# Row sums of 16384 x 1024 floats: one block of 128 rows a partition with one store, in place of blocks of 112 and 16 rows with a store each

## The chip, the cores and the metric

The kernel runs on one core of a Trainium2 chip. Its input lies in HBM, the chip's main memory, and is worked on in SBUF, the memory beside the core's engines, which has 128 partitions; DMA engines move the data between them in packets. SyncE and ScalarE issue these transfers; VectorE and ScalarE do the sums. The metric is device time in microseconds (us); lower is better. A time is some 1.8 us longer than the span of its profile (162.43 against 160.6 us for the profiled run of before), so differences carry over from one to the other.

## The reference

```python
def setup_inputs():
    batch, seq, dim = 32, 512, 1024
    return {"x": np.random.randn(batch, seq, dim).astype(np.float32)}

def reference(x):
    return np.sum(x, axis=-1).astype(np.float32)
```

67.1 MB are read and 64 KB are written. There is one addition for every four bytes read; the profile below shows that the reading sets the time.

## The kernel before

The 16384 rows are dealt to 128 partitions. A *block* with n rows a partition gives partition p the rows p*n to p*n + n - 1 of that block, so neighbouring partitions start n * 4 KiB apart in HBM. This distance is called the *pitch* below. A tile is 16 rows a partition, 64 KiB each, 8.39 MB in all.

```python
BLOCKS = (112, 16)
G = 16                                   # rows a partition in one tile
...
xpool = ctx.enter_context(tc.tile_pool(name="x", bufs=3))
...
def block(r0, n):
    x_b = x_flat[r0 : r0 + P * n].rearrange("(p c) d -> p (c d)", p=P)
    out_b = out_flat[r0 : r0 + P * n].rearrange("(p c) -> p c", p=P)
    return x_b, out_b, rpool.tile([P, n], F32, name=f"res{r0}")

for b, n in enumerate(BLOCKS):
    x_b, out_b, res = block(done * P, n)
    final = b == len(BLOCKS) - 1
    whole = n - G if final else n
    while c < whole:                     # seven whole tiles in all
        ...  # load of 16 rows from SyncE, reduce on VectorE;
        ...  # in the seventh tile ScalarE sums 7 of the 16 rows
    if not final:
        nc.scalar.dma_start(out=out_b, in_=res)      # 112 columns, 448 B a partition
    done += n

# the last tile: loads of 9, 4 and 2 rows and of two parts of a row;
# VectorE and ScalarE share its rows
...
nc.sync.dma_start(out=out_b, in_=res)                # 16 columns, 64 B a partition
```

The seven whole tiles are at a pitch of 448 KiB, the last one, the block of 16 rows, at 64 KiB.

## Time and profile before

| | before |
|---|---|
| time, median of the first 3 runs | 162.22 us (162.12 to 162.32) |
| span of the profile | 160.6 us |
| first whole reduce starts | 22.00 us |
| from one whole reduce to the next | 19.35 us |
| last store issued | 158.36 us |

The page of the kernel before: the span, the two DMA queues (packets, MB, share of the span of 16 engines) and the chain of work that ended last, by engine and by line.

```profile
span 160.6 us, 119 instructions
...
q1 hardware_dynamic: 2016, 67.12, 97.2%
q10 hardware_dynamic: 144, 0.06, 0.1%
...
DMA 75%; DVE 23%; SPq 0%; issue 0%; DVEq 0%
DMA xt<-in_x_dram 75%; DVE res L43 21%; DVE pairs L59 1%; SPq L95 0%; DVE seen L112 0%; DVE part L59 0%; DVE res L59 0%; DVEq L120 0%
...
```

The load queue is busy for 97.2% of the span, and waits for a load make up 75% of the span in the chain. The 23% on VectorE look like a second limit, but the timeline shows that they are not. Here are some of its VectorE lines for before: start, duration, engine, line, operation, operands, and in brackets how long VectorE had been idle and what ended that.

```profile
...
start us, us, engine line op out<-in xcount [idle before <-releaser]
22.00 17.22 DVE L43 TENSOR_REDUCE res<-xt 128x16 f32<-128x16384 f32 x1 [22.00 <-DMA xt<-in_x_dram]
41.27 17.22 DVE L43 TENSOR_REDUCE res<-xt 128x16 f32<-128x16384 f32 x1 [2.06 <-DMA xt<-in_x_dram]
60.63 17.22 DVE L43 TENSOR_REDUCE res<-xt 128x16 f32<-128x16384 f32 x1 [2.13 <-DMA xt<-in_x_dram]
...
138.03 9.75 DVE L43 TENSOR_REDUCE res<-xt 128x9 f32<-128x9216 f32 x1 [2.13 <-DMA xt<-in_x_dram]
...
156.58 0.69 DVE L59 CUSTOM_DVE_ANT_0 pairs<-xt 128x512 f32<-128x512 f32 x1 [0.25 <-DMA xt<-in_x_dram]
...
```

Each whole reduce takes 17.22 us, and then VectorE waits about 2.1 us for the next tile. A tile arrives every 19.35 us, so 8.39 MB / 19.35 us = 434 GB/s. The Trainium skill, "DMA: Bandwidth & Descriptors", section Specifications, gives 435 GB/s as the fabric ceiling, the limit at SBUF's ports; the trace agrees.

The line of the last store in the same timeline, and the list of DMA issues (out<-in, issuing queue, KB, us from issue to landing):

```profile
...
158.36 0.35 SPq L114 DMA_DIRECT2D out_dram<-res  x1
```

```profile
...
issues: line engine op xcount, KB each, median us to landing
xt<-in_x_dram SPq DMA_DIRECT2D x1, 7680.0 KB, 21.5
...
out_dram<-res ACTq DMA_DIRECT2D x1, 56.0 KB, 7.5
out_dram<-res SPq DMA_DIRECT2D x1, 8.0 KB, 1.4
```

### The profile page before, as it was taken

The numbers are of one execution on the slowest core, as the hardware profiler recorded it, in microseconds if no ns is written. First come the engines' busy times: TensorE is split into PE (matmuls) and PEld (weight loads), VectorE is DVE, ScalarE is ACT, GpSimd is POOL, SyncE is SP. The second block draws the span as 40 slices with busy tenths as digits, with TensorE's granted clock in tenths as the row PEclk, the third lists the DMA queues.
The fourth block names the chain that finished last, engine by engine and source line by source line (L and its number), as shares of the span: only waits on it lengthen the run. The fifth ranks groups of instructions, "written<-read, shape, count | busy, mean of one in ns | idle before, by whom it ended". The sixth has DMA issues, their size and how long they took to land.

```text
span 160.6 us, 119 instructions
## 1 busy us (share of the span) xinstructions
DVE 121.5 (76%) x16; ACT 17.2 (11%) x31; POOL 0.2 (0%) x4
## 2 busy tenths in 40 slices
DVE  0000059997799959999499994999949998697884
ACT  0000000000000000000000000000000000695892
POOL 0000000000000000000000000000000000000000
DMA  9988996996996996996996996996996996998991
GB/s 375 490 367 367 490 522 277 506 522 277 506 522 261 522 522 261 522 522 261 522 506 277 522 506 277 522 506 277 522 506 277 522 490 294 441 431 364 436 390 44
DMA packets 2160, 67.18 MB, mean 418 GB/s; under 512 B 496, under 2 KB 624, under 8 KB 880
## 3 DMA queue, kind: packets, MB, share of 16 engines
q1 hardware_dynamic: 2016, 67.12, 97.2%
q10 hardware_dynamic: 144, 0.06, 0.1%
HBM read 67.11 MB, written 0.07 MB: 418 GB/s over the span
## 4 chain that ended last, share of the span: by engine, by line
DMA 75%; DVE 23%; SPq 0%; issue 0%; DVEq 0%
DMA xt<-in_x_dram 75%; DVE res L43 21%; DVE pairs L59 1%; SPq L95 0%; DVE seen L112 0%; DVE part L59 0%; DVE res L59 0%; DVEq L120 0%
## 5 line engine op out<-in xcount | busy, mean ns | idle before, releaser
L43 DVE TENSOR_REDUCE res<-xt 128x16 f32<-128x16384 f32 (+3 forms) x9 | 119.8, 13309 | 36.5 <-DMA xt<-in_x_dram 36.5
L51 ACT ACT_TABLE_LOAD x1 | 1.3, 1283 | 138.1 <-DMA xt<-in_x_dram 138.1
L51 ACT ACTIVATE xt<-xt 128x1024 f32<-128x1024 f32 x15 | 15.6, 1044 | 2.4 <-DMA xt<-in_x_dram 2.3
L51 ACT ACTIVATION_READ_ACCUMULATOR xt<-xt 128x1 f32 x15 | 2.8, 187 | 0.0
L59 DVE CUSTOM_DVE_ANT_0 pairs<-xt 128x512 f32<-128x512 f32 (+1 forms) x2 | 1.1, 567 | 0.2 <-DMA xt<-in_x_dram 0.2
L59 DVE CUSTOM_DVE_ANT_0 pairs<-xt,part 128x240 f32<-128x240 f32 x1 | 0.5, 468 | 0.0
L112 DVE COPY seen<-part 128x1 f32<-128x1 f32 x1 | 0.2, 153 | 0.0
L59 DVE DVE_READ_ACCUMULATOR2_ANT res<- 128x1 f32 x2 | 0.2, 83 | 0.0
L157 POOL MEMSET const-uint8-127<- 128x1 uint8 x1 | 0.1, 102 | 0.0
L157 POOL MEMSET const-bfloat16-1.0<- 128x1 bf16 x1 | 0.1, 101 | 0.0
L157 POOL MEMSET const-float32-0.0<- 128x1 f32 x1 | 0.1, 99 | 0.2 <-issue 0.2
L157 POOL MEMSET const-float32-1.0<- 128x1 f32 x1 | 0.1, 99 | 0.0
L59 DVE DVE_READ_ACCUMULATOR2_ANT part<- 128x1 f32 x1 | 0.1, 83 | 0.0
## 6 DMA issues: line engine op xcount, KB each, us to landing
xt<-in_x_dram SPq DMA_DIRECT2D x1, 7680.0 KB, 21.5
xt<-in_x_dram SPq DMA_DIRECT2D x1, 4608.0 KB, 32.5
xt<-in_x_dram SPq DMA_DIRECT2D x1, 2048.0 KB, 37.1
xt<-in_x_dram SPq DMA_DIRECT2D x1, 1024.0 KB, 39.1
xt<-in_x_dram SPq DMA_DIRECT2D x1, 512.0 KB, 3.8
xt<-in_x_dram SPq DMA_DIRECT2D x1, 272.0 KB, 39.3
xt<-in_x_dram SPq DMA_DIRECT2D x1, 240.0 KB, 39.4
xt<-in_x_dram SPq DMA_DIRECT2D x6, 40.8
```

The lines of the kernel that those rows point to most:

```text
L43: nc.vector.tensor_reduce(out=res[:, c : c + n], in_=xt[:, j * D : (j + n) * D].rearrange("p (j d) -> p j d", d=D), axis=X, op=ADD,)
L51: nc.scalar.activation(out=v, in_=v, func=COPY, accum_out=acc)
L59: nc.vector.tensor_tensor_reduce(out=pairs[:, 0 : h - a], in0=xt[:, a:h], in1=xt[:, h:b], scale=1.0, scalar=first, op0=ADD, op1=ADD, accum ...
L112: nc.vector.tensor_copy(out=seen, in_=part)
L157: nc = _bacc.Bacc("TRN2", target_bir_lowering=False, num_devices=1)
```

## The change

The intent is one DMA less: the results are kept until the end and stored at once, 512 B a partition. The early store no longer runs among the last loads.

```diff
-BLOCKS = (112, 16)
+BLOCKS = (128,)
```

This one line also moves the rows: every tile is now at a pitch of 512 KiB. Which partition sums which row changes, the result doesn't. The tiles, their sizes and the work of each engine stay as they were.

## The prediction

> **What bounds the kernel now.** The loads do. The page gives the load queue 97.2% of the 16 DMA engines' span. The chain of waits is 75% "DMA xt<-in_x_dram". Its 23% on VectorE is not a limit: the timeline shows the 17.22 us tile reduces starting every 19.35 us (41.27, 60.63, 79.97, 99.32 us), each after a 2.13 us wait for a load. A tile is 8.39 MB, so 19.35 us is 434 GB/s. The Trainium skill, "DMA: Bandwidth & Descriptors", section Specifications, gives a fabric ceiling of 435 GB/s; the trace agrees. In the packet records every 64 KiB packet takes 2.42 us (10th to 90th percentile 2.418 to 2.43), in the 112-row block, whose partitions start 448 KiB apart, and in the 16-row block, 64 KiB apart, alike.
>
> **What the change does.**
> 1. It removes the store of 112 columns that ScalarE issued at 147.87 us: 128 packets of 448 B, 8 on each engine, 25 ns each in the packet records. They ran between the last loads and hold each engine for 8 x 25 ns = 0.20 us. The last loads should land 0.20 us earlier; that is on the critical path. The 0.37 us of issue on ScalarE is not: it waits afterwards for a load until 149.07 us.
> 2. It makes the last store 64 KB instead of 8 KB, 512 B a partition instead of 64 B. The 64 B packets take 11 ns. A line through 64 B (11 ns) and 448 B (25 ns) gives 27 ns for 512 B, so 8 packets take 0.22 us instead of 0.09 us: +0.13 us, an estimate, fully exposed after the last reduce. The rest of its 1.4 us from issue to landing stays.
> 3. It moves the rows in HBM. The partitions of every tile now start 512 KiB apart, a power of two. The packets (64 KiB) and all work of VectorE and ScalarE stay the same.
>
> Items 1 and 2 sum to about -0.07 us, below the run-to-run spread (162.12 to 162.32 us).
>
> Item 3 is the risk. The same page, section Latency and other measured facts, reports 207 GB/s for copies between HBM tensors with a row pitch of 512 KiB, against 214 GB/s with a padded pitch, and a far larger loss from 2 MiB on. If that 3% applied to this one-way read, the loads' 155 us would become 160 us, and the kernel would take 167 us. I do not expect it: HBM is only read here, in 64 KiB runs, and the engines seem to set the 2.42 us. No run of this case shows it yet.
>
> **Prediction.** 162.1 us, within 161.7 to 163.4 us 8 times in 10. Faster by over 2%: 1%. Within 2%: 82%. Slower by over 2%: 17%.
>
> **What the profile would show.**
> - Item 1 right: the second DMA queue is gone; the wait of the first pair reduction (156.58 us) ends about 0.2 us earlier, and so does the issue of the last store (158.36 us).
> - Item 2 right: that store goes from 1.4 us to about 1.5 us between issue and landing; the span after its issue (2.3 us) grows by about 0.13 us.
> - Item 3 harmless: 64 KiB packets stay at 2.42 us, tile reduces 19.35 us apart. Harmful: the spacing grows in all tiles alike, towards 20 us, with longer packets and longer waits of VectorE for the loads.
>
> **What would make it wrong.** A loss from the 512 KiB pitch in the reads (slower by 1 to 4%); a last store whose 512 B writes finish much later or sooner than that line says. A gain over 2% would need loads above 434 GB/s, and nothing in the change can give that.

## The result, and the profile after

| | before | after |
|---|---|---|
| time, median of 6 runs each | 162.27 us (162.12 to 162.49) | 162.76 us (162.58 to 162.94) |
| ratio of the times | | 1.003, 95% interval 1.0018 to 1.0043 |

A ratio here is the mean time of one kernel's fast runs over that of the other's of the same rounds, so it is not quite the ratio of the medians. The difference of 0.49 us is small, but clear of the noise.

The page of the kernel after, the same lines:

```profile
span 161.0 us, 118 instructions
...
q1 hardware_dynamic: 2016, 67.18, 97.2%
...
DMA 75%; DVE 22%; SPq 0%; issue 0%; DVEq 0%
DMA xt<-in_x_dram 75%; DVE res L43 21%; DVE pairs L59 1%; SPq L95 0%; DVE seen L112 0%; DVE part L59 0%; DVEq L120 0%; DVE res L59 0%
...
```

The second queue is gone and the shares are the same: the page cannot show where 0.4 us went. The VectorE lines of the timeline can (after):

```profile
...
start us, us, engine line op out<-in xcount [idle before <-releaser]
22.39 17.22 DVE L43 TENSOR_REDUCE res<-xt 128x16 f32<-128x16384 f32 x1 [22.39 <-DMA xt<-in_x_dram]
41.66 17.22 DVE L43 TENSOR_REDUCE res<-xt 128x16 f32<-128x16384 f32 x1 [2.06 <-DMA xt<-in_x_dram]
61.02 17.22 DVE L43 TENSOR_REDUCE res<-xt 128x16 f32<-128x16384 f32 x1 [2.14 <-DMA xt<-in_x_dram]
...
138.43 9.75 DVE L43 TENSOR_REDUCE res<-xt 128x9 f32<-128x9216 f32 x1 [2.13 <-DMA xt<-in_x_dram]
...
156.72 0.69 DVE L59 CUSTOM_DVE_ANT_0 pairs<-xt 128x512 f32<-128x512 f32 x1 [0.20 <-DMA xt<-in_x_dram]
...
```

```profile
...
158.54 0.35 SPq L114 DMA_DIRECT2D out_dram<-res  x1
```

```profile
...
issues: line engine op xcount, KB each, median us to landing
xt<-in_x_dram SPq DMA_DIRECT2D x1, 7680.0 KB, 21.9
...
out_dram<-res SPq DMA_DIRECT2D x1, 64.0 KB, 1.5
```

The first whole reduce starts 0.39 us later. From there everything keeps pace: 41.66 to 61.02 us is again a spacing of about 19.35 us. At the end some of the delay comes back. Four stretches make up the span: S up to the start of the first whole reduce, M from there to the reduce of 9 rows, E from there to the issue of the last store, T from there to the end of the span. Their sums differ from the span by rounding only.

| us | S | M | E | T | span |
|---|---|---|---|---|---|
| before | 22.00 | 116.03 | 20.33 | 2.29 | 160.65 |
| after | 22.39 | 116.04 | 20.11 | 2.49 | 161.03 |

So the start costs 0.39 us, E gains 0.22 us, T costs 0.20 us, and the 116 us in the middle, six tiles at full rate, do not change at all.

The packet records of the DMA engines show the start finer. Of the first tile, one row comes in packets of 4 KiB, and then the other 15 rows as one DMA, in packets of 60 KiB, eight rounds of one packet on each of the 16 engines. The packets sorted by start, in groups of 16, mean duration in us, from both traces:

```
                    round 1  round 2  round 3  round 4   packets over 2.3 us
before                 2.27     2.27     2.27     2.27     0 of 128
after                  2.63     2.40     2.39     2.27    30 of 128
```

After the change the first three rounds are slow, and from the fourth on the packets take 2.27 us as before. The very first packets, of 4 KiB, differ too: before, the first six started 0, 5, 14, 17, 18 and 46 ns after the earliest, and after the change 0, 55, 103, 172, 224 and 282 ns. (The records do not name the engine of a packet; a round here is only the order of the starts.)

### The profile page after: what moved, and what is told of

Same layout as the page of the kernel before. It is cut to its first block, busy times and chain, and to the rows that moved or that the text cites. A ratio compares the mean times of both kernels' runs of the same rounds, so it can differ in the third digit from the quotient of the medians.

```text
span 161.0 us, 118 instructions
## 1 busy us (share of the span) xinstructions
DVE 121.5 (75%) x16; ACT 17.1 (11%) x31; POOL 0.2 (0%) x4
## 4 chain that ended last, share of the span: by engine, by line
DMA 75%; DVE 22%; SPq 0%; issue 0%; DVEq 0%
DMA xt<-in_x_dram 75%; DVE res L43 21%; DVE pairs L59 1%; SPq L95 0%; DVE seen L112 0%; DVE part L59 0%; DVEq L120 0%; DVE res L59 0%
```

## The experiments

**Theory A:** the pitch of 512 KiB makes the loads collide as long as all engines start together, and only then; the stores nearly cancel. Rivals: **N**, the late first tile was the luck of one profile; **S**, the larger last store costs the 0.5 us; **F**, only the first touch of HBM is slow; **B**, something else in the block of 128 rows costs it, not its pitch.

Twelve kernels ran. They ran in four batches, each on another chip: late_store, blocks_64_64, one_buffer_before and one_buffer_after in one, the two at 508 KiB in one, the two at 448 KiB in one, the rest in one. The kernel before was timed again in each, at medians of 162.27 to 162.32 us, and the ratios are taken within a batch; comparisons of one-buffer kernels at 508 or 448 KiB with the other two cross chips. First the stretches of all profiles with three buffers:

| us | pitch, KiB | early store | last store, B a partition | S | M | E | T | median time, ratio to before |
|---|---|---|---|---|---|---|---|---|
| before | 448, 64 | among loads | 64 | 22.00 | 116.03 | 20.33 | 2.29 | 1 |
| store_only | 448, 64 | among loads | 64 | 22.03 | 116.03 | 20.22 | 2.29 | 162.23, 0.9990 |
| late_store | 448, 64 | after loads | 64 | 21.83 | 116.03 | 20.11 | 2.29 | 162.23, 0.9991 |
| blocks_96_32 | 384, 128 | among loads | 128 | 21.99 | 116.04 | 20.21 | 2.31 | 162.34, 0.9996 |
| blocks_64_64 | 256 | in mid run | 256 | 22.00 | 116.10 | 20.11 | 2.33 | 162.39, 1.0009 |
| pitch_448 | 448 | none | 512 | 21.91 | 116.04 | 20.12 | 2.49 | 162.34, 1.0006 |
| after | 512 | none | 512 | 22.39 | 116.04 | 20.11 | 2.49 | 162.76, 1.0030 |
| after_again | 512 | none | 512 | 22.31 | 116.03 | 20.12 | 2.49 | 162.80, 1.0026 |
| pitch_only | 512 | among loads | 64 | 22.05 | 116.03 | 20.22 | 2.30 | 162.67, 1.0020 |
| pitch_508 | 508 | none | 512 | 22.09 | 116.03 | 20.13 | 2.49 | 162.59, 1.0020 |

In the six profiles with a first pitch of 448 KiB or less, S lies between 21.83 and 22.03 us: a difference of 0.2 us in one profile's S means nothing by itself.

### after_again: the changed kernel once more

No edit.

> The changed kernel once more, for a second profile. In its first profile the first tile reduce began at 22.39 us instead of 22.00, all later tiles kept 19.35 us of spacing, the last store was issued 0.18 us later than before and the span after its issue was 2.46 instead of 2.28 us. Theory A (the 512 KiB pitch collides only while the loads start): the first tile reduce begins at 22.3 us or later again, with 60 KiB packets of 2.4 to 2.9 us in the first two or three rounds of packets, and the time is 0.3 to 0.6 us over before. Rival N (the late first tile was the luck of one profile): it begins at 22.0 us, and the 0.5 us has to be found elsewhere. Rival S (the larger last store costs the 0.5 us): the tail after its issue is 0.4 us or more longer than before.

Measured: 162.80 us (162.54 to 163.11, 6 runs), ratio 1.0026, interval 1.0011 to 1.0041. Two VectorE lines of its timeline:

```profile
...
22.31 17.22 DVE L43 TENSOR_REDUCE res<-xt 128x16 f32<-128x16384 f32 x1 [22.31 <-DMA xt<-in_x_dram]
...
138.34 9.75 DVE L43 TENSOR_REDUCE res<-xt 128x9 f32<-128x9216 f32 x1 [2.13 <-DMA xt<-in_x_dram]
...
```

The first tile is late again, S = 22.31 us, with 22 of 128 packets over 2.3 us, 21 of them in the first two rounds. Rival N falls. T is 2.49 us once more, 0.20 us longer than before (the expectation's 2.46 and 2.28 us come from rounded spans; the records give 2.49 and 2.29), not by 0.4 us or more, so rival S can be a part of it at most.

### pitch_only: the rows moved, both stores kept

```diff
-        x_b = x_flat[r0 : r0 + P * n].rearrange("(p c) d -> p (c d)", p=P)
-        out_b = out_flat[r0 : r0 + P * n].rearrange("(p c) -> p c", p=P)
+        c0 = r0 // P
+        x_b = x_flat.rearrange("(p c) d -> p (c d)", p=P)[:, c0 * D : (c0 + n) * D]
+        out_b = out_flat.rearrange("(p c) -> p c", p=P)[:, c0 : c0 + n]
```

> The 512 KiB pitch alone: rows lie as in the changed kernel, but the two stores, 112 columns from ScalarE during the last loads and 16 columns at the end, stay as before. Theory A: first tile reduce at 22.3 us or later, still 0.3 to 0.4 us late at the issue of the last store (which is issued at about 158.7 us, since the early store still holds up the last loads), tail after the issue 2.3 us as before; time 0.3 to 0.6 us over before. Rivals N and S: the time of before, within 0.15 us.

Measured: 162.67 us (162.38 to 163.01), ratio 1.0020, interval 1.0005 to 1.0035: over before with the stores of before. Its profile, though, is a partial miss:

```profile
...
22.05 17.22 DVE L43 TENSOR_REDUCE res<-xt 128x16 f32<-128x16384 f32 x1 [22.05 <-DMA xt<-in_x_dram]
...
138.08 9.76 DVE L43 TENSOR_REDUCE res<-xt 128x9 f32<-128x9216 f32 x1 [2.12 <-DMA xt<-in_x_dram]
...
```

S is 22.05 us, not 22.3 or later. The slow packets are there (20 of 128 over 2.3 us, the first rounds at 2.50 and 2.35 us on average), but in this execution the last of these packets ended only 0.06 us later than in before (21.61 against 21.54 us), and the tile is complete only when it has. The profiled execution was the quickest of the six (162.38 us; the others took 162.62 to 163.01). As M, E and T agree to 0.02 us in all profiles with the same stores (but for the E of before itself, told under store_only), I take the others' extra time to be in S; their profiles were not kept, so this is inferred. What is shown is that the loss at the start varies from one profile to the next.

### store_only and late_store: the early store moved behind the loads

The first attempt only moved the statement behind ScalarE's last row:

```diff
-            nc.scalar.dma_start(out=out_b, in_=res)
+            early = (out_b, res)
...
     rows_act(xt, res, 14, 1, c + 14)
+    nc.scalar.dma_start(out=early[0], in_=early[1])
```

> The stores alone: rows lie as before (448 KiB and 64 KiB), but the store of 112 columns is issued by ScalarE after its last row, about 157.5 us, when the loads have landed, so that it no longer runs among them; the store of 16 columns stays. Theory A: first tile reduce at 22.0 us; the last loads land 0.2 us earlier and the last store is issued at about 158.16 instead of 158.36 us; time 0.1 to 0.2 us under before, and under the changed kernel by 0.5 us or more. Rival S: about the time of before or more, since the bytes stored at the end are those of the changed kernel. If the end of the program waits for the early store too, the tail after the last store may grow by up to 0.2 us and the gain vanish.

It failed as an experiment: the scheduler moved the store back in front of the rows (presumably since its data were ready earlier). ScalarE's queue in the timeline of store_only:

```profile
...
147.90 0.37 ACTq L109 DMA_DIRECT2D out_dram<-res  x1
...
```

That is before's 147.87 us again. So the run is a repeat of before, and useful as such: 162.23 us (162.10 to 162.38), ratio 0.9990, interval 0.9976 to 1.0004. It also corrects a number: its E is 20.22 us, as in two other runs whose early store runs among the last loads, where the profile of before had 20.33. Of the 0.22 us that E seemed to gain, 0.11 us were therefore a matter of that one profile of before, which has some slow packets in the last tile's first load (36 KiB packets of 1.40 to 1.47 us on average in three rounds, against 1.36). That these packets made the difference was not tested.

The second attempt forced the order:

```diff
-    rows_act(xt, res, 14, 1, c + 14)
+    last_row = sum_act(xt[:, 14 * D : 15 * D], res[:, c + 14 : c + 15])
+    with tc.issue_after(last_row.ins):
+        nc.scalar.dma_start(out=early[0], in_=early[1])
```

> What store_only was meant to be (there ScalarE's store was still issued at 147.90 us, since the scheduler moved it back to its old place, so that run was a repeat of before): rows as before, the store of 112 columns forced behind ScalarE's last row, at about 157.6 us. The loads are then free of its packets: the first pair reduction starts at about 156.3 us instead of 156.5, the last store is issued at about 158.1 us. The 8 packets of 448 B an engine run at about 158.6 to 158.8 us, before the last store's packets at about 159 us. Theory A: time 0.1 to 0.2 us under before, 0.5 us or more under the changed kernel. Rival S (64 KB stored at the end cost the 0.5 us): at or above the time of before by 0.3 us or more.

Its timeline: ScalarE's queue, SyncE's last store, and two VectorE lines.

```profile
...
156.23 0.37 ACTq L110 DMA_DIRECT2D out_dram<-res  x1
...
```

```profile
...
157.98 0.35 SPq L116 DMA_DIRECT2D out_dram<-res  x1
```

```profile
...
21.83 17.22 DVE L43 TENSOR_REDUCE res<-xt 128x16 f32<-128x16384 f32 x1 [21.83 <-DMA xt<-in_x_dram]
...
137.87 9.75 DVE L43 TENSOR_REDUCE res<-xt 128x9 f32<-128x9216 f32 x1 [2.13 <-DMA xt<-in_x_dram]
...
```

The early store is issued at 156.23 us, just after ScalarE's last row has begun (156.17 us) and not after its end as expected; its packets run from 157.10 us, when the loads have ended (157.00 us), and end 1.4 us before the last store's first one. E is 20.11 us: taking the early store out of the loads is worth 0.11 us against 20.22. T is 2.29 us, as in before: nothing is paid at the end. The time is 162.23 us (162.06 to 162.28, 5 runs), ratio 0.9991, interval 0.9979 to 1.0003. That is under the changed kernel's 162.76 to 162.80 us, as theory A has it, and rival S's increase of 0.3 us does not come. Against before the gain is no more than a tendency. It is the version to keep, if any.

### blocks_96_32 and blocks_64_64: smaller pitches

```diff
-BLOCKS = (112, 16)
+BLOCKS = (96, 32)        # in the other: (64, 64)
```

> Both kernels' code with blocks of 96 and 32 rows: pitch of 384 KiB, then 128 KiB, a store in the middle of the run (among loads) and one of 32 columns (128 B) at the end. Theory A, if it is the 512 KiB pitch: first tile reduce at 22.0 us, time of before within 0.15 us. If the start is slow here too, it is not the power of two but any pitch other than 448 KiB, or luck.

> Both kernels' code with two blocks of 64 rows: a pitch of 256 KiB throughout, also a power of two, with a store of 64 columns in mid run and one of 64 columns (256 B a partition) at the end. If any large power of two collides at the start: first packets of 60 KiB over 2.3 us and first tile reduce after 22.1 us, time 0.2 to 0.6 us over before. If 256 KiB is small enough: first tile reduce at 22.0 us and the time of before within 0.15 us.

Measured: 162.34 us (162.13 to 162.49), ratio 0.9996, interval 0.9983 to 1.0010, for 96 and 32 rows; 162.39 us (162.04 to 163.08), ratio 1.0009, interval 0.9992 to 1.0026, for 64 and 64. S is 21.99 and 22.00 us, and neither has a 60 KiB packet over 2.3 us. A pitch of 256 KiB, also a power of two, starts cleanly in its one profile.

### one_buffer_before and one_buffer_after: every tile starts on idle engines

```diff
-    xpool = ctx.enter_context(tc.tile_pool(name="x", bufs=3))
+    xpool = ctx.enter_context(tc.tile_pool(name="x", bufs=1))
```

With one buffer, the load of a tile cannot start before the reduce of the tile before has ended, so the start happens eight times.

> The kernel before with one buffer for the tiles of x instead of three, so that every tile's load starts on idle DMA engines, when the reduce of the tile before has ended. A reference for one_buffer_after: about 300 us, every tile load of 8 MB landing about 21 us after its issue, packets of 64 KiB at 2.42 us throughout, also in the first rounds of each tile.

> The changed kernel with one buffer: the suspected cost, made to happen at every tile. Theory A (512 KiB pitch collides whenever all engines start together): every tile lands 0.2 to 0.5 us later than in one_buffer_before, with slow 64 KiB packets (over 2.6 us) in the first two or three rounds of each tile; time 1.5 to 4 us above one_buffer_before. Rival F (only the first touch after the launch is slow): the first tile late by 0.3 to 0.4 us, all others as in one_buffer_before; 0.3 to 0.6 us above it. Rival N: no difference beyond 0.3 us.

Measured: 293.68 us (two runs, 293.58 and 293.79) against 296.43 us (296.06 and 296.80): 2.75 us more. The view of waits, first of one_buffer_before and then of one_buffer_after (us in total, times, longest):

```profile
...
engine line waited for: us in total, times, longest us
...
DVE res L43 <- DMA xt<-in_x_dram: 167.9, 9, 22.1
...
```

```profile
...
engine line waited for: us in total, times, longest us
...
DVE res L43 <- DMA xt<-in_x_dram: 170.7, 9, 22.4
...
```

VectorE waits 2.8 us longer for loads, and T adds 0.2 us; the spans are 292.0 and 295.0 us. Three of the tiles in the timelines, before and then after:

```profile
...
61.22 17.22 DVE L43 TENSOR_REDUCE res<-xt 128x16 f32<-128x16384 f32 x1 [21.99 <-DMA xt<-in_x_dram]
100.46 17.22 DVE L43 TENSOR_REDUCE res<-xt 128x16 f32<-128x16384 f32 x1 [22.03 <-DMA xt<-in_x_dram]
139.45 17.22 DVE L43 TENSOR_REDUCE res<-xt 128x16 f32<-128x16384 f32 x1 [21.77 <-DMA xt<-in_x_dram]
...
```

```profile
...
61.68 17.22 DVE L43 TENSOR_REDUCE res<-xt 128x16 f32<-128x16384 f32 x1 [22.44 <-DMA xt<-in_x_dram]
101.22 17.22 DVE L43 TENSOR_REDUCE res<-xt 128x16 f32<-128x16384 f32 x1 [22.32 <-DMA xt<-in_x_dram]
140.85 17.22 DVE L43 TENSOR_REDUCE res<-xt 128x16 f32<-128x16384 f32 x1 [22.41 <-DMA xt<-in_x_dram]
...
```

Over the six whole tiles after the first the wait is 22.37 us on average against 21.95 us: 0.42 us a start. Rival F falls; it had the loss in the first tile alone, which here started alike (22.01 and 22.02 us, the same spread as in pitch_only). The expectation of "packets of 2.42 us in the first rounds" too was wrong: in one_buffer_before the first round of 64 KiB packets takes about 3.1 us (2.95 to 3.14 on average), so an idle start has a cost of its own at every pitch tried.

The other part of the expectation, packets over 2.6 us in the second and third rounds, was a near miss: there are four and two in the first two of these tiles and none in the other four. The packets' starts tell the pitches apart more steadily. A packet takes over 2.4 us here, so the first 16 of a tile come from the 16 different engines. On average they start 0.40 to 0.42 us after the earliest in all six tiles of one_buffer_after, against 0.16 to 0.33 us in one_buffer_before and 0.13 to 0.18 us in one_buffer_448 below. So part of the 0.42 us is that the engines begin later; the rest is spread over slower packets here and there.

### pitch_508 and one_buffer_508: all of the changed kernel, at another pitch

```diff
-        x_b = x_flat[r0 : r0 + P * n].rearrange("(p c) d -> p (c d)", p=P)
+        x_b = bass.AP(x_flat.tensor, x_flat.offset, [[127 * D, P], [1, n * D]])
```

Every instruction stays, only addresses change. The sums are wrong, since neighbours share rows.

> The changed kernel with every instruction the same, except that the partitions of x start 127 rows (508 KiB) apart instead of 128 rows (512 KiB); neighbours then share rows, so the sums are wrong on purpose. Theory A (the pitch of 512 KiB alone makes the start slow): packets of 60 KiB at 2.27 us from the first round on (at most one or two over 2.3 us), first tile reduce at 21.8 to 22.05 us, time within 0.15 us of before and 0.4 to 0.5 us under the changed kernel. Rival B (something else in the block of 128 rows costs it, such as the larger store or the one DMA queue): time of the changed kernel, 162.6 to 162.9 us.

> The same 508 KiB pitch with one buffer, wrong sums on purpose. Theory A: as one_buffer_before, 293.5 to 294.0 us, each whole tile waiting 21.7 to 22.1 us for its load, and 64 KiB packets over 2.46 us in the first round of a tile only (about 16 a tile). Rival B: as one_buffer_after, 296 to 297 us, with waits of 22.3 to 22.4 us.

Measured: 162.59 us (162.32 to 162.69, 5 runs), ratio 1.0020, interval 1.0007 to 1.0034; and 296.40 us (296.30 and 296.49). Theory A as it stood, that only the pitch of 512 KiB is slow, falls: the time of one_buffer_508 is that of one_buffer_after. The profiles look different, however. In pitch_508 only 1 of 128 packets of 60 KiB is over 2.3 us. In one_buffer_508 most waits are close to the reference, and one tile is 1.6 us late. Its waits, and two tiles of its timeline:

```profile
...
engine line waited for: us in total, times, longest us
...
DVE res L43 <- DMA xt<-in_x_dram: 170.4, 9, 23.7
...
```

```profile
...
100.40 17.22 DVE L43 TENSOR_REDUCE res<-xt 128x16 f32<-128x16384 f32 x1 [21.95 <-DMA xt<-in_x_dram]
...
220.19 17.22 DVE L43 TENSOR_REDUCE res<-xt 128x16 f32<-128x16384 f32 x1 [23.73 <-DMA xt<-in_x_dram]
...
```

So 508 KiB loses time in another way: less regularly, here in a few packets of one tile (five after its first round are over 2.46 us). Both executions lost about 2.7 us, but only one of them has a profile, and with three buffers the interval of pitch_508 overlaps that of pitch_448 below. That 508 KiB is slow rests on little.

### pitch_448 and one_buffer_448: all of the changed kernel, at the pitch of before

```diff
-        x_b = bass.AP(x_flat.tensor, x_flat.offset, [[127 * D, P], [1, n * D]])
+        x_b = bass.AP(x_flat.tensor, x_flat.offset, [[112 * D, P], [1, n * D]])
```

(The lines on the left are those of pitch_508.) Again wrong sums. This is the run that decides between theory A and rival B.

> Every instruction of the changed kernel, with the partitions of x 112 rows (448 KiB) apart in all tiles, as in the big block of before; sums wrong on purpose. The run at 508 KiB left it open: its packets started cleanly, yet it took 0.3 us more than before. If a wide pitch is what costs, and 508 KiB still has some of it (theory A, no longer bound to the power of two): first tile reduce at about 22.0 us, only the net of the two stores is left (0.12 us gained, 0.17 us lost), time within 0.15 us of before. If the stores or the one queue cost it (rival B): 0.3 us or more over before, as at 508 KiB.

> The same with one buffer. Theory A: 293.5 to 294.2 us, as one_buffer_before, with waits of about 22.0 us before each whole tile. Rival B (something other than the layout of the loads makes the one-buffer kernels take 296.4 us): 296 us or more.

Measured: 162.34 us (162.34 to 162.56, 5 runs), ratio 1.0006, interval 0.9992 to 1.0020; and 293.67 us (293.45 to 293.87, 4 runs), against 293.68 of one_buffer_before. The first reduce and the last store of pitch_448, and then the waits of one_buffer_448:

```profile
...
21.91 17.22 DVE L43 TENSOR_REDUCE res<-xt 128x16 f32<-128x16384 f32 x1 [21.91 <-DMA xt<-in_x_dram]
...
```

```profile
...
158.07 0.35 SPq L114 DMA_DIRECT2D out_dram<-res  x1
```

```profile
...
engine line waited for: us in total, times, longest us
...
DVE res L43 <- DMA xt<-in_x_dram: 167.8, 9, 22.2
...
```

With the changed kernel's instructions, its one queue and its one store, a pitch of 448 KiB gives back the time of before, to 0.01 us with one buffer. E and T are those of the changed kernel (20.12 and 2.49 us); only S differs, 21.91 us against 22.31 and 22.39. Rival B falls: the loss comes with the addresses of the loads. And half of the 0.20 us in T, which pitch_448 also has, is covered by the 0.11 us in E, so that rival S is left with about 0.1 us.

## Why the prediction was right or wrong

The prediction said "within 2%", at 162.1 us with a range of 161.7 to 163.4 us; 162.76 us lies inside. Its main reading held: the loads set the pace, at the ceiling, and the stores are worth tenths of a microsecond. The small difference has the other sign, +0.49 us in place of -0.07 us. Its terms:

1. *"The last loads should land 0.20 us earlier."* Right in mechanism, mis-sized: 0.11 us, from E of 20.21 to 20.22 us in three runs with the early store among the last loads and 20.11 to 20.13 us in the runs without it. Comparing the two kernels' first profiles alone would have confirmed the 0.20 us (E fell by 0.22), by luck. The packets take 25 ns as it said; that 8 of them delay the last loads by their whole 0.20 us was not so.
2. *"+0.13 us"* for the larger last store: right for the store, but T grew by 0.20 us (2.29 to 2.30 against 2.49 us). The 512 B packets take the 27 ns of the estimate, and from issue to landing the store takes 1.41 us at 64 B and 1.55 us at 512 B, +0.14 us, as forecast (1.43 us at 128 B, 1.45 us at 256 B). The other 0.06 us come after the landing, where nothing was forecast: from there to the end of the span it is 0.88 us in all profiles with two stores and 0.94 us in all with one. In the instruction records SyncE, which closes the program with a series of waits on semaphores, has five of them left after the landing in place of four, about 0.06 us apart. No run has one small store, or a 512 B store beside an early one, so size and number of stores are not separated by an experiment.
3. *"Item 3 harmless"*, for the pitch of 512 KiB: this is the step that failed, and the largest term. In the steady state it is harmless, M is 116.03 to 116.04 us at 448 and 512 KiB. While the loads start, it costs 0.3 to 0.4 us in two of three profiles with three buffers, and 0.42 us a start on average with one buffer. The prediction did fear the pitch, but expected its harm *"in all tiles alike"*, with the spacing growing towards 20 us. It looked at the rate of a stream that runs, not at the start.

The sum fits: +0.3 to 0.4 us at the start, -0.11 us in E, +0.2 us in T, is 0.4 to 0.5 us, where the medians differ by 0.49 us, and by 0.48 us in after_again (162.80 against 162.32).

What stays open: why the wide pitch is slow at a start. The engines begin later there, 0.40 to 0.42 us after the earliest on average with one buffer, the first few packets in ones and twos about 50 ns apart; what holds them back, no run shows. At 508 KiB that average is 0.13 to 0.36 us and time is lost all the same, so a second cause may be at work. Whether it is the distance of the partitions or the range of addresses that a tile spans (it is 512 KiB times 128 in the one case and 448 KiB times 128 in the other) was not separated, nor was a pitch between 448 and 508 KiB tried.

## What to carry to other kernels

When a change of tiling touches a stream that runs at its ceiling, split the span into start, steady state and end before reading anything into a difference: here all of it was outside the steady state, and the page's shares, equal in both kernels, could not show it. A block size is also an address pattern: to tell the two apart, keep every instruction and change the stride alone, and multiply the suspected cost (one buffer makes eight starts of one). And one profile is one execution: a stretch that agrees with the forecast to 0.02 us was half luck.

## What the Trainium skill lacked or had wrong

- "DMA: Bandwidth & Descriptors", section Latency and other measured facts, the row on HBM row pitch, has 207 GB/s at 512 KiB against 214 GB/s for copies between HBM tensors. For loads from HBM into SBUF this case shows no loss of steady rate at 512 KiB (a tile of 8.39 MB every 19.35 us, 434 GB/s, as at 448 KiB), and a loss at starts of the stream instead, which the row lacks: 0.42 us on average over six starts with one buffer.
- The same row advises padding the pitch by a few KiB (+4 KiB restored the full rate there, at a pitch of 4 MiB). Here, 508 KiB, which is 4 KiB less than 512 KiB, did not restore the time: 296.40 us with one buffer (two runs), against 296.43 us at 512 KiB and 293.67 us at 448 KiB. A padded pitch of 516 KiB was not run.
- No section that I found gives the time of a small last store from SyncE by its size. Here, from issue to landing: 1.41 us with 64 B a partition, 1.43 with 128 B, 1.45 with 256 B, 1.55 with 512 B; and then 0.88 to 0.94 us to the end of the span. The section Specifications puts the smallest transfer for line rate at 512 B; no run here tests that for a last store, since the store of 512 B a partition also moved the most bytes.
